# Weights that begin at eleven offsets, and activation blocks 1040 bytes apart

## The chip, the cores and the metric

The kernel runs on one core of one Trainium2 chip. The metric is device time in microseconds of that core, the median of several runs. One execution of the kernel before was profiled, and all rows shown here are from it.

## The reference, cut to what matters

One decoder layer over 256 tokens of width 1024, all in float32. What is computed:

```
h      = rmsnorm(x) ;  q, k, v, u_pool, gate_logits = split(h @ w_in)
attn   = causal attention over q, k (per-head norm, partial rotary), v
pooled = four trailing-mean poolings of u_pool, then a small map
mixed  = sig(g0) * (attn @ w_branch_attn) + sig(g1) * (pooled @ w_branch_pool)
x      = x + mixed @ w_out
up     = causal_depthwise_conv(rmsnorm(x) @ w_up)          # 1024 -> 2 * 2816
out    = x + (silu(up_gate) * up_value) @ w_down           # 2816 -> 1024
```

## The kernel before

Every large product is made of three float32r products: an operand is split into a high part (ScalarE, `high`, L78) and a low part, the difference (VectorE, `low`, L82 or L84), and TensorE adds high·high, high·low and low·high in PSUM (`mm3`, L90 to L92; the same in `down`, L632 to L634, and `project`, L276).

Weights come in chunks of 128 partitions by 2048 numbers (8192 bytes per partition). SyncE loads a chunk into one of four `raw` buffers. `next_high` writes its high part into one of four `whi` buffers and `next_low` the low part into one of four `wlo` buffers, each in two pieces of 1024 columns. The list `order` sets the order of the chunks: q, k, v, p (pooling input), g (gates, 8 chunks), the pool maps, bp and ba (branches), o (output, 4 chunks), then up (22 chunks) mixed with dn (11 chunks).

Activations lie transposed, as 8 blocks (`k`) of 256 tokens: `xhi` and `xlo` for the first half, `hhi` and `hlo` in the same buffers for the feed-forward part. In p, g, o, up and dn a weight tile of 128 by 128 is the stationary operand (an LDWEIGHTS, then the MATMUL), and 256 columns of activations move past it. A chunk of g, o, up or dn is used by 48 such matmuls: g, o and up by 2 feature tiles of 8 blocks and 3 products, dn by 2 rows of blocks, 8 tiles and 3 products. In q, k and v the operands change places: 128 tokens are stationary and 512 weight columns move.

In the built program the buffers follow one another without gaps that matter here: each `whi` and `wlo` buffer begins 64 bytes past a multiple of 128, each tile in it a multiple of 512 bytes later; `xhi`, `xlo` and all other activation operands begin 96 bytes past a multiple of 128, and their blocks are 1024 bytes apart. So before the change every float32r matmul with 256 columns meets one pair of residues modulo 128: 64 for the weights, 96 for the activations.

The program's order on each engine is the order in which the code issues it. After the normalised keys are made, GpSimd does the rotary part of q and k in `norm_evacuate` (L294 to L305), with scratch tiles `ra` and `rb` of two buffers each.

Of the kernel before, what the change touches and what calls it, by code (L numbers as in the profile page):

```python
# [8 lines left out]
F32 = mybir.dt.float32  # L9
F32R = mybir.dt.float32r  # L10
# [4 lines left out]
P = 128  # L15
S = 256
NT = S // P
D = 1024
KD = D // P
H = 8  # L20
# [8 lines left out]
ROPE = 16  # L29
# [3 lines left out]
CH = 2048  # L33
# [17 lines left out]
STAGGER = 1  # L51
AHEAD = 4
FFN_AHEAD = 6
XCUTS = (1, 2, 4, 6, 8)


@with_exitstack
def hybrid_layer_kernel(ctx: ExitStack, tc: tile.TileContext, xq_d, par_d, wkv_d, wpg_d,
# [5 lines left out]
    whi_p = ctx.enter_context(tc.tile_pool(name="whi", bufs=WBUFS))  # L64
    wlo_p = ctx.enter_context(tc.tile_pool(name="wlo", bufs=WBUFS))
    act = ctx.enter_context(tc.tile_pool(name="act", bufs=1))
# [4 lines left out]
    tmp = mixer.enter_context(tc.tile_pool(name="tmp", bufs=2))  # L71
# [5 lines left out]
    def high(hi, src, scale=1.0):  # L77
        nc.scalar.activation(hi, src, AF.Copy, scale=scale)  # L78
# [16 lines left out]
    order = [("q", None)] * 2 + [("k", wkv_d[c]) for c in range(2)]  # L95
# [10 lines left out]
    raws, his, los = {}, {}, {}  # L106
# [14 lines left out]
    def raw(c, sl):  # L121

        return xq[:, 4 * c + sl.start // 512, S:] if order[c][0] == "q" else raws[c][:, sl]
# [10 lines left out]
    def oldest():  # L134

        return next((c for c in range(len(order)) if c not in spent), len(order))

    def next_high():
        if at[0] < len(pieces):
            c, sl, first, _ = pieces[at[0]]  # L140
            if c - oldest() >= WBUFS:
                return
            at[0] += 1
            if first:
                his[c] = whi_p.tile([P, CH], F32R, tag="whi", name=f"hi_{order[c][0]}{c}")
                los[c] = wlo_p.tile([P, CH], F32R, tag="wlo", name=f"lo_{order[c][0]}{c}")
            high(his[c][:, sl], raw(c, sl))

    def next_low(eager=False):
# [9 lines left out]
    def ahead(upto=0):  # L159

        next_high()
        next_low()
        if at[1] - sum(p[0] < used[0] for p in pieces) < upto:
            next_high()
            next_low()
# [14 lines left out]
    gmix = xq_all[:, 0:KD]  # L180
    xq = xq_all[:, KD:].rearrange("p (k c) -> p k c", c=S + AW)
    xT = xq[:, :, 0:S]
    xhi = act.tile([P, KD, S], F32R, tag="xhi", name="xhi")
    xlo = act.tile([P, KD, S], F32R, tag="xlo", name="xlo")
    par = const.tile([P, C_END], F32, name="par")
    scrap = const.tile([P, 1], F32, name="scrap")
    nc.scalar.activation(scrap, ones[:, 0:1], AF.Copy)
# [1 line left out]
    cut = 0  # L189
    for k in XCUTS:  # L190
        end = KD + k * (S + AW)
# [25 lines left out]
    for k in range(KD):  # L217
        if k == 0:
            nc.vector.tensor_scalar(xhi[:, k, :], xT[:, k, :], gmix[:, k:k + 1], None, op0=ALU.mult)
        else:  # L220
            high(xhi[:, k, :], xT[:, k, :], gmix[:, k:k + 1])
        low(xlo[:, k, :], xhi[:, k, :], xT[:, k, :], gmix[:, k:k + 1])
        next_high()
        next_low(eager=True)
# [56 lines left out]
    def norm_evacuate(pt, t, gcol, name):  # L281
        r = rtok1[:, t:t + 1]
        g = par[:, None, gcol:gcol + DH].to_broadcast([P, H, DH])
        p3 = pt.rearrange("p (h d) -> p h d", d=DH)
        qg = tmp.tile([P, 2, 3 * P], F32, tag="big", bufs=4, name=f"qg_{name}{t}")
        qg = qg.rearrange("p a b -> p (a b)")[:, 0:AW].rearrange("p (h d) -> p h d", d=DH)
        q2 = tmp.tile([P, H, DH], F32, tag="q2", bufs=1, name=f"q2_{name}{t}")
        nc.scalar.activation(q2, p3, AF.Square, scale=r)
        nc.vector.scalar_tensor_tensor(qg, p3, r, g, ALU.mult, ALU.mult)
        ss = tmp.tile([P, H], F32, tag="ss", name=f"ss_{name}{t}")  # L290
        nc.vector.tensor_reduce(ss, q2, axis=AX.X, op=ALU.add)
        nc.vector.tensor_scalar(ss, ss, 1.0 / DH, EPS, op0=ALU.mult, op1=ALU.add)
        rh = tmp.tile([P, H], F32, tag="rh", name=f"rh_{name}{t}")
        nc.gpsimd.tensor_tensor(rh, ss, mhalf[:, 0:H], ALU.pow)  # L294
        nc.gpsimd.tensor_tensor(qg, qg, rh[:, :, None].to_broadcast([P, H, DH]), ALU.mult)
        cos = par[:, None, C_COS + t * ROPE:C_COS + (t + 1) * ROPE].to_broadcast([P, H, ROPE])
        sin = par[:, None, C_SIN + t * ROPE:C_SIN + (t + 1) * ROPE]
        ta = tmp.tile([P, H, ROPE], F32, tag="ropea", name=f"ra_{name}{t}")
        tb = tmp.tile([P, H, ROPE], F32, tag="ropeb", name=f"rb_{name}{t}")
        nc.gpsimd.tensor_tensor(ta, qg[:, :, 0:ROPE], cos, ALU.mult)  # L300
        nc.gpsimd.tensor_tensor(tb[:, :, 0:HALF], qg[:, :, HALF:ROPE],
                                sin[:, :, 0:HALF].to_broadcast([P, H, HALF]), ALU.mult)
        nc.gpsimd.tensor_tensor(tb[:, :, HALF:ROPE], qg[:, :, 0:HALF],
                                sin[:, :, HALF:ROPE].to_broadcast([P, H, HALF]), ALU.mult)
        nc.gpsimd.tensor_tensor(qg[:, :, 0:ROPE], ta, tb, ALU.add)  # L305
        return qg
# [18 lines left out]
    def on_k(k):  # L325
        if k % 2 == 1:
            ahead()
        if k == 3:
            stat.append(ps2.tile([P, 2, 512], F32, tag="ps2", name="ps_n1"))
            token_rms(stat[0][:, 0, :], x2, rtok1, "n1")  # L330
            diagonal(rtok1)
            qg.append(norm_evacuate(ptq[0], 0, C_QG, "q"))
        if k == 5:
            qg.append(norm_evacuate(ptq[1], 1, C_QG, "q"))
        if k == 6:
            spread_rms(stat[0][:, 1, 0:S], R1)

    def on_v(k):
        if k % 2 == 1:
            ahead()  # L340
        if k == 1:
            kg.append(norm_evacuate(ptk[0], 0, C_KG, "k"))
        if k == 3:
            kg.append(norm_evacuate(ptk[1], 1, C_KG, "k"))
# [152 lines left out]
    for n in range(2 * KD):  # L497
# [5 lines left out]
        b, c = n // 2, n % 2  # L503
# [30 lines left out]
    tmp = ctx.enter_context(tc.tile_pool(name="ffn", bufs=2))  # L534
# [14 lines left out]
    low(ml[:, KD - 1, :], mh[:, KD - 1, :], gate(KD - 1))  # L549


    hhi = act.tile([P, KD, S], F32R, tag="xhi", name="hhi")
    hlo = act.tile([P, KD, S], F32R, tag="xlo", name="hlo")
    ss2 = tmp.tile([P, S], F32, tag="ss2", bufs=1, name="ss2")

    def tile_part(w, opers, c, ps, ks):
# [56 lines left out]
    def value_done(i, g, uc):  # L613
        taps(uc[0], KF + i, uc[1])
        nc.gpsimd.tensor_tensor(uc[1], g[1], uc[1], ALU.mult)  # L615
        acch[i] = tmp.tile([P, S], F32R, tag="ah", bufs=LAG + 2, name=f"ah{i}")
        accl[i] = tmp.tile([P, S], F32R, tag="al", bufs=LAG + 2, name=f"al{i}")
        high(acch[i], uc[1])
        return uc[1]
# [4 lines left out]
    def down(i, ms):  # L624
        if i % 2 == 0 and i // 2 not in wd:
            wd[i // 2] = chunk("dn")
        hi, lo = wd[i // 2]
        for m in ms:
            sl = slice((i % 2) * D + m * P, (i % 2) * D + (m + 1) * P)
            o = acc[m // 2][:, (m % 2) * S:(m % 2 + 1) * S]  # L630
            first = i == 0 and m % 2 == 0
            nc.tensor.matmul(o, hi[:, sl], acch[i], start=first, stop=False, skip_group_check=True)  # L632
            nc.tensor.matmul(o, hi[:, sl], accl[i], start=False, stop=False, skip_group_check=True)  # L633
            nc.tensor.matmul(o, lo[:, sl], acch[i], start=False, stop=i == KF - 1, skip_group_check=True)  # L634
        if i % 2 == 1 and len(ms) == KD:
            spent.add(next(c for c in his if his[c] is hi))
# [29 lines left out]
    for i in range(1, KF):  # L666
# [11 lines left out]
        if i >= LAG:  # L678
# [4 lines left out]
            down(i - LAG, range(KD))  # L683
            ahead(FFN_AHEAD)
        done = value_done(i, ug, uv)
# [6 lines left out]
    for m in (0, 2, 4, 6, 1, 3, 5, 7):  # L692
        for i in (KF - 2, KF - 1):
            down(i, (m,))
        o = acc[m // 2][:, (m % 2) * S:(m % 2 + 1) * S]
# [75 lines left out]
```

## Time and profile before

| What | us |
|---|---|
| median of 3 runs | 358.66 |
| lowest and highest of them | 357.54, 359.63 |
| the profiled execution's own time | 356.89 |
| its span, first to last instruction | 355.1 |

The span is what the rows below add up to; about 1.8 us of the execution lie around it. "PE" is TensorE's matmuls and "PEld" its weight loads, which overlap them; "DVE" is VectorE, "ACT" ScalarE, "POOL" GpSimd. A matmul's duration in a row is its way through the array, so neighbours overlap; what a matmul costs in a dense stretch is the distance from one start to the next.

### The profile page before, as it was taken

How to read it: one execution, taken by the hardware profiler on the slowest of the kernel's cores; microseconds unless marked ns; L12 is line 12 of the kernel's file. 1: busy time of each engine (PE TensorE's matmuls, PEld its weight loads, DVE VectorE, ACT ScalarE, POOL GpSimd, SP SyncE). 2: the span in 40 equal slices, each digit the busy share in tenths (PEclk: the TensorE clock that was granted, in tenths of full speed). 3: DMA queues.
4: the chain of work that ended last, by engine and by line, in shares of the span. 5: the costliest groups of instructions: out<-in, count | busy, mean ns of one | idle time of the engine just before them, and what ended most of it. 6: DMA issues, size and time to landing. Idle time of an engine off the chain costs nothing.

```text
span 355.1 us, 6775 instructions
## 1 busy us (share of the span) xinstructions
PE 344.3 (97%) x2760; PEld 334.5 (94%) x2760; DVE 255.3 (72%) x401; ACT 195.4 (55%) x311; POOL 101.7 (29%) x127
## 2 busy tenths in 40 slices
PE   8999895999999999999999999999999999999996
PEld 6887794999999999999999999999999999999996
DVE  4879727944677597499789986667777777777743
ACT  5955614636464984566467565555555555556420
POOL 1008999100000006379232222121212121212140
PEclk9999998999999999999999999999999999999999
DMA  7985623244263464075534764646455453642003
GB/s 281 420 341 178 252 90 119 49 173 170 116 236 120 173 258 163 6 293 194 221 117 140 278 236 180 220 145 231 134 222 185 172 228 128 238 132 107 2 0 118
DMA packets 10254, 62.76 MB, mean 177 GB/s; under 512 B 1136, under 2 KB 2288, under 8 KB 3312
## 3 DMA queue, kind: packets, MB, share of 16 engines
q1 hardware_dynamic: 10224, 62.34, 48.3%
q8 instruction: 21, 0.34, 0.4%
q14 instruction: 9, 0.07, 0.1%
HBM read 61.29 MB, written 1.05 MB: 176 GB/s over the span
## 4 chain that ended last, share of the span: by engine, by line
PE 75%; POOL 8%; DVE 8%; DMA 3%; ACT 2%; issue 2%; SPq 1%; POOLq 0%
PE ps_up L91 11%; PE ps_up L90 11%; PE ps_up L92 11%; PE ps_d L633 6%; PE ps_d L632 6%; PE ps_d L634 6%; PE ps_g L90 5%; PE ps_g L91 4%; PE ps_g L92 4%; DMA raw_k<-in_wkv 3%; DVE lo_up L82 2%; DVE hlo L84 2%; POOL rh_k L294 1%; POOL rh_q L294 1%; PE ps_bp L90 1%
## 5 line engine op out<-in xcount | busy, mean ns | idle before, releaser
L91 PE MATMUL ps_up<-hlo,hi_up 128*128 128x256 f32 x352 | 98.5, 280 | 0.2 <-DVE hlo L84 0.2
L90 PE MATMUL ps_up<-hhi,hi_up 128*128 128x256 f32 x352 | 98.7, 280 | 0.0
L92 PE MATMUL ps_up<-hhi,lo_up 128*128 128x256 f32 x352 | 98.4, 280 | 0.0
L91 PEld LDWEIGHTS ps_up<-hlo,hi_up 128*128 128x128 f32 x352 | 66.2, 188 | 0.4 <-DVE hlo L84 0.4
L90 PEld LDWEIGHTS ps_up<-hhi,hi_up 128*128 128x128 f32 x352 | 66.2, 188 | 0.0
L92 PEld LDWEIGHTS ps_up<-hhi,lo_up 128*128 128x128 f32 x352 | 66.2, 188 | 0.0
L82 DVE TENSOR_TENSOR lo_up<-raw_up,hi_up 128x1024 fp32r<-128x1024 f32 x44 | 55.9, 1274 | 6.1 <-ACT hi_up L78 6.1
L615 POOL TENSOR_TENSOR c_v<-c_g,c_v 128x256 f32<-128x256 f32 x22 | 16.3, 740 | 120.7 <-DVE c_v L598 120.7
L633 PE MATMUL ps_d<-al,hi_dn 128*128 128x256 f32 x176 | 49.2, 280 | 0.0
L634 PE MATMUL ps_d<-ah,lo_dn 128*128 128x256 f32 x176 | 49.2, 280 | 0.0
L632 PE MATMUL ps_d<-ah,hi_dn 128*128 128x256 f32 x176 | 49.2, 279 | 0.0
L78 ACT ACTIVATE hi_up<-raw_up 128x1024 fp32r<-128x1024 f32 x44 | 44.9, 1045 | 0.0
L90 PE MATMUL ps_g<-xhi,hi_g 128*128 128x256 f32 x128 | 37.5, 293 | 0.0
L91 PE MATMUL ps_g<-xlo,hi_g 128*128 128x256 f32 x128 | 36.3, 284 | 0.0
L92 PE MATMUL ps_g<-xhi,lo_g 128*128 128x256 f32 x128 | 36.3, 284 | 0.0
L78 ACT ACTIVATE ah<-c_v 128x256 fp32r<-128x256 f32 x22 | 9.2, 418 | 45.9 <-POOL c_v L615 45.9
L634 PEld LDWEIGHTS ps_d<-ah,lo_dn 128*128 128x128 f32 x176 | 33.1, 188 | 0.0
L632 PEld LDWEIGHTS ps_d<-ah,hi_dn 128*128 128x128 f32 x176 | 33.1, 188 | 0.0
L633 PEld LDWEIGHTS ps_d<-al,hi_dn 128*128 128x128 f32 x176 | 33.1, 188 | 0.0
L545 POOL TENSOR_TENSOR xq<-xq 128x256 f32<-128x256 f32 x8 | 7.0, 887 | 74.1 <-issue 70.1
L82 DVE TENSOR_TENSOR lo_dn<-raw_dn,hi_dn 128x1024 fp32r<-128x1024 f32 x22 | 27.8, 1265 | 0.4 <-ACT hi_dn L78 0.4
L603 DVE TENSOR_TENSOR u_v<-ps_up,R 128x256 f32<-128x256 f32 x22 | 9.3, 422 | 26.1 <-PE ps_up L92 26.1
(191 smaller groups left out, 843.7 us busy)
## 6 DMA issues: line engine op xcount, KB each, us to landing
raw_up<-in_wup SPq DMA_DIRECT2D x22, 1024.0 KB, 4.8
raw_dn<-in_wdn SPq DMA_DIRECT2D x11, 1024.0 KB, 4.8
raw_g<-in_wpg SPq DMA_DIRECT2D x8, 1024.0 KB, 4.8
raw_o<-in_wout SPq DMA_DIRECT2D x4, 1024.0 KB, 4.8
xq<-in_xq SPq DMA_DIRECT2D x3, 768.0 KB, 7.3
raw_v<-in_wkv SPq DMA_DIRECT2D x2, 1024.0 KB, 14.0
raw_p<-in_wpg SPq DMA_DIRECT2D x2, 1024.0 KB, 6.3
raw_bp<-in_wbp SPq DMA_DIRECT2D x2, 1024.0 KB, 5.5
```

The costliest lines, as they stand in the source:

```text
L78: nc.scalar.activation(hi, src, AF.Copy, scale=scale)
L82: nc.vector.tensor_tensor(lo, src, hi.bitcast(F32), ALU.subtract)
L84: nc.vector.scalar_tensor_tensor(lo, src, scale, hi.bitcast(F32), ALU.mult, ALU.subtract)
L90: nc.tensor.matmul(out, sh, mh, start=start, stop=False, **kw)
L91: nc.tensor.matmul(out, sh, ml, start=False, stop=False, **kw)
L92: nc.tensor.matmul(out, sl, mh, start=False, stop=stop, **kw)
L294: nc.gpsimd.tensor_tensor(rh, ss, mhalf[:, 0:H], ALU.pow)
L603: nc.vector.tensor_tensor(u, ps[:, 0:S], R2, ALU.mult)
L615: nc.gpsimd.tensor_tensor(uc[1], g[1], uc[1], ALU.mult)
L632: nc.tensor.matmul(o, hi[:, sl], acch[i], start=first, stop=False, skip_group_check=True)
L633: nc.tensor.matmul(o, hi[:, sl], accl[i], start=False, stop=False, skip_group_check=True)
L634: nc.tensor.matmul(o, lo[:, sl], acch[i], start=False, stop=i == KF - 1, skip_group_check=True)
```

## The change

Each `whi` and `wlo` buffer grows by 112 bytes, and the chunk inside begins at one of eleven byte offsets, 0, 64, 4, 32, 8, 96, 16, 48, 80, 112 or 12, by its turn among the chunks of its name. Only chunks of up, dn, g and o are shifted; the high and the low part of a chunk take the same offset. In the built program a buffer takes 8320 bytes, so buffers still begin 64 past a multiple of 128, and the offset adds to that. The activation tiles `xhi`, `xlo`, `hhi` and `hlo` get blocks of 260 numbers, of which 256 are used, so that block `k` begins 16·k bytes later than before modulo 1024. The rotary scratch tiles go from two buffers to one each, which makes room.

```
+SHIFT = (0, 64, 4, 32, 8, 96, 16, 48, 80, 112, 12)
+SPAN = S + 4
...
             if first:
-                his[c] = whi_p.tile([P, CH], F32R, tag="whi", name=f"hi_{order[c][0]}{c}")
-                los[c] = wlo_p.tile([P, CH], F32R, tag="wlo", name=f"lo_{order[c][0]}{c}")
+                name = order[c][0]
+                turn = sum(order[i][0] == name for i in range(c))
+                off = SHIFT[turn % len(SHIFT)] // 4 if name in ("up", "dn", "g", "o") else 0
+                his[c] = whi_p.tile([P, CH + max(SHIFT) // 4], F32R, tag="whi", name=f"hi_{name}{c}")[:, off:off + CH]
+                los[c] = wlo_p.tile([P, CH + max(SHIFT) // 4], F32R, tag="wlo", name=f"lo_{name}{c}")[:, off:off + CH]
...
-    xhi = act.tile([P, KD, S], F32R, tag="xhi", name="xhi")
-    xlo = act.tile([P, KD, S], F32R, tag="xlo", name="xlo")
+    xhi = act.tile([P, KD, SPAN], F32R, tag="xhi", name="xhi")[:, :, 0:S]
+    xlo = act.tile([P, KD, SPAN], F32R, tag="xlo", name="xlo")[:, :, 0:S]
...
-        ta = tmp.tile([P, H, ROPE], F32, tag="ropea", name=f"ra_{name}{t}")
-        tb = tmp.tile([P, H, ROPE], F32, tag="ropeb", name=f"rb_{name}{t}")
+        ta = tmp.tile([P, H, ROPE], F32, tag="ropea", bufs=1, name=f"ra_{name}{t}")
+        tb = tmp.tile([P, H, ROPE], F32, tag="ropeb", bufs=1, name=f"rb_{name}{t}")
...
-    hhi = act.tile([P, KD, S], F32R, tag="xhi", name="hhi")
-    hlo = act.tile([P, KD, S], F32R, tag="xlo", name="hlo")
+    hhi = act.tile([P, KD, SPAN], F32R, tag="xhi", name="hhi")[:, :, 0:S]
+    hlo = act.tile([P, KD, SPAN], F32R, tag="xlo", name="hlo")[:, :, 0:S]
```

The change moves no instruction: on every engine the built program holds the same instructions in the same order with the same semaphore waits, at other addresses. The one place where a wait could have been added is GpSimd's queue, where the rotary part's scratch tiles lose their second buffer. GpSimd's rows there, before (`ra_q` and `rb_q` are the scratch tiles, `qg_q` a half of the queries):

```order
L300 TENSOR_TENSOR ra_q_289<-qg_q_279,par 128x128 [waits DMAHW7_49,Pool_49]
L301 TENSOR_TENSOR rb_q_290<-qg_q_279,par 128x8x8
L303 TENSOR_TENSOR rb_q_290<-qg_q_279,par 128x8x8
L305 TENSOR_TENSOR qg_q_279<-ra_q_289,rb_q_290 128x8x16 [waits Pool_49]
L294 TENSOR_TENSOR rh_q_320<-ss_q_317,mhalf 128x8 [waits DVE_49]
L295 TENSOR_TENSOR qg_q_313<-qg_q_313,rh_q_320 128x512 [waits Pool_49]
L300 TENSOR_TENSOR ra_q_323<-qg_q_313,par 128x128 [waits Pool_49]
```

The same place in the changed program, whose lines stand six further down:

```order
L306 TENSOR_TENSOR ra_q_289<-qg_q_279,par 128x128 [waits DMAHW7_49,Pool_49]
L307 TENSOR_TENSOR rb_q_290<-qg_q_279,par 128x8x8
L309 TENSOR_TENSOR rb_q_290<-qg_q_279,par 128x8x8
L311 TENSOR_TENSOR qg_q_279<-ra_q_289,rb_q_290 128x8x16 [waits Pool_49]
L300 TENSOR_TENSOR rh_q_320<-ss_q_317,mhalf 128x8 [waits DVE_49]
L301 TENSOR_TENSOR qg_q_313<-qg_q_313,rh_q_320 128x512 [waits Pool_49]
L306 TENSOR_TENSOR ra_q_323<-qg_q_313,par 128x128 [waits Pool_49]
```

Only the line numbers differ: the second use of the scratch tiles waits for GpSimd's own earlier work in both.

## Rows read from the trace of the kernel before

**Rows 1.** The page's first part: busy us, share of the span, instructions.

```profile
PE 344.3 (97%) x2760; PEld 334.5 (94%) x2760; DVE 255.3 (72%) x401; ACT 195.4 (55%) x311; POOL 101.7 (29%) x127
```

**Rows 2.** Busy time by stretch: length, engines, TensorE's granted clock, DMA.

```profile
core 0: us, PE busy (x) PEld busy (x) DVE busy (x) ACT busy (x) POOL busy (x), PEclk, DMA share, GB/s
70.00:130.00 60.00, 60.00 (x519) 59.34 (x518) 38.58 (x66) 36.38 (x72) 0.00 (x0) 1.00 0.47 169
130.00:177.00 47.00, 46.41 (x394) 45.95 (x393) 37.39 (x58) 24.62 (x36) 26.35 (x24) 1.00 0.52 189
177.00:345.00 168.00, 168.00 (x1442) 168.00 (x1441) 125.62 (x188) 96.06 (x144) 39.21 (x44) 1.00 0.46 164
```

**Rows 3.** Timeline of TensorE, feed-forward: start, duration, instruction; 1152 starts apart.

```profile
200.46 0.28 PE L90 MATMUL ps_up<-hhi,hi_up 128*128 128x256 f32 x1
...
334.86 0.28 PE L90 MATMUL ps_up<-hhi,hi_up 128*128 128x256 f32 x1
```

**Rows 4.** Timeline of TensorE in the k projection, pairs with 512 columns.

```profile
18.48 0.63 PE L276 MATMUL ps_k<-hi_k,xhi 128*128 128x512 f32 x2
18.95 0.63 PE L276 MATMUL ps_k<-hi_k,xlo 128*128 128x512 f32 x2
...
21.75 0.63 PE L276 MATMUL ps_k<-hi_k,xlo 128*128 128x512 f32 x2
```

**Rows 5.** Timeline of TensorE early in the gates; nine starts apart.

```profile
61.10 0.41 PE L92 MATMUL ps_g<-xhi,lo_g 128*128 128x256 f32 x1
...
63.02 0.42 PE L92 MATMUL ps_g<-xhi,lo_g 128*128 128x256 f32 x1
```

**Rows 6.** Busy time around the gates' first tile, columns as in rows 2.

```profile
54.00:59.00 5.00, 1.27 (x12) 1.03 (x10) 4.43 (x9) 3.33 (x6) 4.77 (x8) 1.00 0.53 184
61.00:63.00 2.00, 2.00 (x11) 2.00 (x11) 1.93 (x4) 0.00 (x0) 1.87 (x5) 0.50 0.00 0
```

**Rows 7.** Timeline of TensorE in the pooling input; 88 starts apart.

```profile
43.04 0.28 PE L91 MATMUL ps_u<-xlo,hi_p 128*128 128x256 f32 x1
...
53.41 0.28 PE L92 MATMUL ps_u<-xhi,lo_p 128*128 128x256 f32 x1
```

**Rows 8.** Weight loads by line and form: busy us, mean ns, idle before.

```profile
L90 PEld LDWEIGHTS ps_up<-hhi,hi_up 128*128 128x128 f32 x352 | 66.2, 188 | 0.0
L276 PEld LDWEIGHTS ps_k<-hi_k,xlo 128*128 128x128 f32 x16 | 3.0, 188 | 0.7
L445 PEld LDWEIGHTS ps_p<-ident,sm 128*128 128x128 f32 x24 | 2.7, 140 | 0.0
```

**Rows 9.** VectorE operations by line and form, columns as in rows 8.

```profile
L598 DVE SCALAR_TENSOR_TENSOR c_v<-u_v,par,c_v 128x254 f32<-128x254 f32 x22 | 10.6, 484 | 0.8
L597 DVE SCALAR_TENSOR_TENSOR c_v<-u_v,par,c_v 128x255 f32<-128x255 f32 x22 | 10.5, 479 | 0.0
L84 DVE SCALAR_TENSOR_TENSOR xlo<-xq,xhi 128x256 fp32r<-128x256 f32 x8 | 3.9, 482 | 1.0 <-ACT xhi L78 0.9
```

**Rows 10.** The chain that ended last, output projection: start, us, what.

```profile
147.91 0.44 DVE xq L564
...
152.43 0.43 issue
152.86 0.84 DVE hlo L84
...
154.48 1.06 ACT hi_o L78
...
157.81 0.33 DVE xq L564
158.15 1.13 DVE lo_up L82
```

## The prediction

> **What bounds the kernel now.** I read the page's busy shares first: TensorE is busy 97% of the span, VectorE 72%, ScalarE 55% [rows 1]. A busy TensorE is not yet a bound, so I read the stretches next. From 70 to 130 us and from 177 to 345 us TensorE has no idle time at all, and from 130 to 177 us it lacks 0.6 us [rows 2]. In 275 of 355 us, then, the time is the number of matmuls times the distance between their starts. Everything else is hidden as long as buffers are filled in time.
>
> So the distance is what to look at. In the feed-forward part two starts that are 1152 matmuls apart (16 rounds of 72: two up tiles of 24 and a down step of 24) lie 134.40 us apart: 116.67 ns each [rows 3]. At the granted full clock, 2.4 GHz, that is 280 cycles for 256 columns, 24 more than one per column. In the k projection with 512 columns, seven pairs take 21.75 − 18.48 = 3.27 us, or 233.6 ns per matmul, 561 cycles, 49 more than one per column [rows 4]. While the clock is granted at half, 1.2 GHz, after TensorE had been busy for 1.27 of 5 us [rows 6], nine starts take 1.92 us: 213.3 ns, which is 256 cycles and none over [rows 5]. The reader is to see three things: there is a loss of 9.4% per column at full clock; it doubles when the columns double, though there is one weight load in either case; at half clock it is gone.
>
> **What the change does, part by part.**
>
> *Instructions and waits.* None is added, removed or reordered on any engine, SyncE's transfers included, and GpSimd's rotary steps wait as before. Losing the second scratch buffer costs 0: both uses stand in one engine's queue, and the second never began before the first had ended.
>
> *Addresses that TensorE reads.* Matmuls with a new address in at least one operand: g 384 and p 96 (re-spaced activations), o 144 (three of four chunks are shifted; mixed activations are not re-spaced), up 1056 (re-spaced), dn 480 (ten of eleven chunks). That is 2160 of 256 columns. The 144 matmuls of q, k and v only get a re-spaced stationary operand; each has a slot of 233 ns for a load that takes 188 ns [rows 4, 8], so I cost them at 0.
>
> What a new residue does to the distance between starts no row shows: in this trace every operand begins at a multiple of 32 bytes. I bound it. From below: the loss goes away, and the distance becomes half of the half-clock distance, 213.3 / 2 = 106.7 ns [rows 5]. That is −10.0 ns × 2160 = −21.6 us. From above: an access that does not begin on a 16-byte multiple runs at half rate, as the half-clock rows do, 213.3 ns. Offsets 4, 8 and 12 are such; they fall on 2 chunks of g, 1 of o, 6 of up and 3 of dn, 12 chunks with 48 matmuls each: 576 × 96.7 ns = +55.7 us. A price between comes from the one stretch at full clock that departs from 116.67: in the pooling input 88 starts take 10.37 us, 117.8 ns each [rows 7]. Its 1.1 ns on all 2160 matmuls would be +2.5 us.
>
> I take 0, for two reasons. First, the loss follows the moving columns and not the loads: a collision of weight reads with activation reads that costs a fixed amount per load would be the same 10 ns at 512 columns, and it is 20 [rows 3, 4]. The moving operand is read straight through 1024 or 2048 bytes, so it passes all residues wherever it begins; a new start can alter the edges, not the middle. Second, in k the residues are exchanged (weights move, activations stand), and the loss per column is the same within the rounding of the rows.
>
> The Trainium skill ("TensorE: Matmul & The Clock Gate", section Back-to-back issue gap) gives a distance of columns / 2.4 plus 2.5 ns for a warm stream, 109.2 ns at 256 columns; the trace disagrees, with 116.67 ns [rows 3]. By that page 7.5 ns per matmul are to be had, and if residues were what withholds them, the sum would be an estimated −16 us. The same skill ("SBUF — State Buffer", section Who interferes with whom) says that TensorE reads its moving operand and its weights through two ports that are independent, which speaks against such a gain; the 512-column rows agree with that, as the loss is not one per load.
>
> *Addresses that VectorE and ScalarE use.* They write the shifted chunks and re-spaced blocks. VectorE's taps already read and write 4 bytes (L597) and 8 bytes (L598) off: 479 and 484 ns, against 482 ns for the low part of a block that begins on a 32-byte multiple [rows 9]. So VectorE: 0. ScalarE has no odd start in the trace. Its cover is wide in the feed-forward part, where it is busy 96 of 168 us and VectorE 126 [rows 2]. Without cover it would count only in the output projection, where a chain of ScalarE and VectorE runs beside TensorE from 147.9 to 174 us [rows 10]; there one chunk of o and one of up have offset 4, four ScalarE passes of 1.06 us, so even 20% more is 0.8 us. I take 0, with 0 to +0.8 as bounds; a gain is excluded, since these passes have no loss that alignment explains.
>
> The sum: 356.9 us for the profiled execution (355.1 of span and 1.8 around it) plus 0. That execution was 1.8 us below the median of the three runs, so as a median I say 358.6 us.
>
> **The rivals.**
>
> *Slower: odd starts stretch the weight loads.* A load takes 188 ns and must begin every 116.67 ns [rows 3, 8], so loads already overlap, and how much of the slot one occupies is not shown. If it is nearly all, an extra access at each odd start pushes the slot. For it: 188 ns is more than the 140 ns of the transposes' loads [rows 8], so loads of this kind are not at their fastest, and 117.8 ns in the pooling input shows that the slot can be pushed. Against it: the load is 188 ns in k too, where the slot is twice as long, so nothing squeezes it now. It decides from 1.8 us, which is 0.83 ns on all 2160 matmuls or 3.1 ns on the 576 with odd starts. Small form, the 1.1 ns above: 358.6 + 2.5 = 361. Large form, half rate on odd starts: 358.6 + 55.7 = 414.
>
> The Trainium skill ("Advanced Engine Details and Errata", section SBUF Cachelines) speaks for this rival: memory lines have 16 bytes, and at least two hits on a line are needed to hide its latency, so a start 4 or 12 bytes off leaves a line with a single hit at one end. No row here shows it.
>
> *Faster: the residues did collide.* All 256-column matmuls meet the pair 64 and 96, and the loss is there in all of them. If it belongs to that pair, most of the new pairs escape it. All of it gives 358.6 − 21.6 = 337; half of the pairs gives 348. For it: a steady 9.4% with no other cause named in the trace. Against it: the two reasons above.
>
> *The change does nothing to what TensorE fetches.* That is my forecast.
>
> **How the numbers follow.** About 0.5%, 1.8 us, is what a measurement of this kernel can tell from no change; its three runs span 2.1 us. My forecast, no change: 0.62, at 358.6, between 357 and 360.4. Slower: 0.24, of which 0.12 the small form up to 368, and 0.12 beyond it. Faster: 0.14, of which 0.06 down to 352 and 0.08 beyond. The range of 352 to 368 holds 0.62 + 0.12 + 0.06 = 0.80. The one likeliest case would have 357 to 360.4 alone.
>
> **What would show it.** In the profile after: the distance between matmul starts in up and dn, chunk by chunk. If I am right, all eleven offsets show 116.67 ns, the loads 188 ns, and the high and low passes their old durations. If odd starts cost, the up chunks of turn 2, 4, 10, 13, 15 and 21 show a longer distance than their neighbours, and nothing else does. If the residues collided, the distances fall, and differ between offsets or between blocks of one tile. The forecast is wrong if the mean distance in the feed-forward part moves by more than 0.8 ns; and if the distance holds but the time moves, the output projection's chain is where to look.

## The result, and the profile after

The changed kernel took 361.06 us (median of 5 runs, 359.84 to 361.24) against 358.48 us (357.54 to 359.63) for the kernel before: a ratio of 1.0066, 95% interval 1.0038 to 1.0094. It is slower by 0.66%, where no change was forecast. The profiled execution took 359.84 us with a span of 358.1 us, 3.0 us more than before.

The page's first part of the changed kernel answers to [rows 1]; the three stretches after it (columns as in [rows 2], their limits moved with the work) answer to [rows 2].

```profile
PE 347.5 (97%) x2760; PEld 338.3 (94%) x2760; DVE 255.1 (71%) x401; ACT 195.5 (55%) x311; POOL 102.5 (29%) x127
```

```profile
70.00:130.00 60.00, 60.00 (x513) 59.34 (x512) 37.83 (x65) 35.90 (x72) 0.00 (x0) 1.00 0.45 165
130.00:178.00 48.00, 47.60 (x402) 47.34 (x401) 38.18 (x60) 25.15 (x37) 26.34 (x24) 1.00 0.53 189
178.00:348.00 170.00, 170.00 (x1441) 170.00 (x1441) 125.21 (x187) 96.09 (x144) 39.81 (x44) 1.00 0.46 162
```

The counts of instructions are the same, and TensorE is the only engine that works clearly longer, by 3.2 us. It is still never idle in the long stretches: in the first it gets through 513 matmuls instead of 519, and in the last the same work takes 2 us more. So the distance from start to start has grown. TensorE's timeline shows it at the same two matmuls as [rows 3], 1152 starts apart:

```profile
201.40 0.28 PE L93 MATMUL ps_up<-hhi,hi_up 128*128 128x256 f32 x1
...
337.57 0.28 PE L93 MATMUL ps_up<-hhi,hi_up 128*128 128x256 f32 x1
```

136.17 us for 1152, or 118.20 ns each, where it was 116.67. On the 1584 matmuls of up and dn these 1.53 ns are 2.4 us of the 3.0. The new distance from start to start is not one number. The last two chunks of dn, in the same timeline, first of offset 112, then of offset 12 (only the first of each three matmuls is shown; 24 starts lie between the first two rows, 27 between the others):

```profile
345.70 0.28 PE L638 MATMUL ps_d<-ah,hi_dn 128*128 128x256 f32 x1
...
348.50 0.28 PE L638 MATMUL ps_d<-ah,hi_dn 128*128 128x256 f32 x1
...
351.01 0.28 PE L638 MATMUL ps_d<-ah,hi_dn 128*128 128x256 f32 x1
...
354.25 0.28 PE L638 MATMUL ps_d<-ah,hi_dn 128*128 128x256 f32 x1
```

That is 116.7 ns in one chunk and 120.0 ns in the next. Chunk means, taken from the starts in the same trace: offsets 4 (o, 119.9 ns) and 16 (dn, 119.8 ns) are as slow as 12, and 8 (dn, 117.7 ns) is faster than 16, so multiples of 16 are not spared. Every other group is as before; the groups by line and form, which answer to [rows 8, 9]:

```profile
L93 PEld LDWEIGHTS ps_up<-hhi,hi_up 128*128 128x128 f32 x352 | 66.2, 188 | 0.0
L604 DVE SCALAR_TENSOR_TENSOR c_v<-u_v,par,c_v 128x254 f32<-128x254 f32 x22 | 10.6, 483 | 0.8
L85 DVE TENSOR_TENSOR lo_up<-raw_up,hi_up 128x1024 fp32r<-128x1024 f32 x44 | 55.8, 1273 | 6.1 <-ACT hi_up L81 6.1
L81 ACT ACTIVATE hi_up<-raw_up 128x1024 fp32r<-128x1024 f32 x44 | 44.9, 1045 | 0.0
```

The weight loads still take 188 ns, and VectorE and ScalarE write the shifted chunks in 1273 and 1045 ns (1274 and 1045 before).

### The profile page after: what moved, and what is told of

Read it like the earlier page. It is cut to its first block, busy times and chain, and to the rows that moved or that the text cites. A ratio compares the mean times of both kernels' runs of the same rounds, so it can differ in the third digit from the quotient of the medians.

```text
span 358.1 us, 6775 instructions
## 1 busy us (share of the span) xinstructions
PE 347.5 (97%) x2760; PEld 338.3 (94%) x2760; DVE 255.1 (71%) x401; ACT 195.5 (55%) x311; POOL 102.5 (29%) x127
## 4 chain that ended last, share of the span: by engine, by line
PE 75%; POOL 8%; DVE 8%; DMA 3%; ACT 2%; issue 2%; SPq 1%; POOLq 0%
PE ps_up L94 11%; PE ps_up L95 11%; PE ps_up L93 11%; PE ps_d L639 6%; PE ps_d L640 6%; PE ps_d L638 6%; PE ps_g L93 5%; PE ps_g L95 4%; PE ps_g L94 4%; DMA raw_k<-in_wkv 3%; DVE lo_up L85 2%; DVE hlo L87 2%; POOL rh_k L300 1%; POOL rh_q L300 1%; PE ps_bp L93 1%
## 5 line engine op out<-in xcount | busy, mean ns | idle before, releaser
L85 DVE TENSOR_TENSOR lo_up<-raw_up,hi_up 128x1024 fp32r<-128x1024 f32 x44 | 55.8, 1273 | 6.1 <-ACT hi_up L81 6.1
L81 ACT ACTIVATE hi_up<-raw_up 128x1024 fp32r<-128x1024 f32 x44 | 44.9, 1045 | 0.0
```

The costliest lines, as they stand in the source:

```text
L85: nc.vector.tensor_tensor(lo, src, hi.bitcast(F32), ALU.subtract)
```

## The experiments

The theory after this: a matmul's moving stream and the next weight load meet in the memory, and the *distance* of their addresses (weight minus moving address, modulo 256) sets how often. The rival: only starts off a multiple of 16 bytes cost. From here on a distance in bytes, or a bare number such as 224, is the one between addresses; in ns it is the one from start to start.

**The change in parts.** Three kernels: the first two are edits of the changed kernel and keep its single scratch buffers, the last takes the activation spacing alone into the kernel before.

```
# e_pad: the larger weight buffers alone
-SPAN = S + 4
+SPAN = S
-off = SHIFT[turn % len(SHIFT)] // 4 if name in ("up", "dn", "g", "o") else 0
+off = 0 if name in ("up", "dn", "g", "o") else 0

# e_shift: larger buffers and offsets
-SPAN = S + 4
+SPAN = S

# e_space, from the kernel before
+SPAN = S + 4
-xhi = act.tile([P, KD, S], F32R, tag="xhi", name="xhi")
+xhi = act.tile([P, KD, SPAN], F32R, tag="xhi", name="xhi")[:, :, 0:S]
...
```

> The larger weight buffers alone: no chunk is shifted inside, activations 1024 bytes apart, so buffers begin 8320 bytes apart and high and low parts no longer have one residue modulo 1024. Theory: part of the loss comes back, +0.5 to +1.5 us against before, with distances of 117 to 118.8 ns in some chunks. Rival (odd starts): 0, all distances 116.67 ns.

Ratio 1.0020 (1.0003 to 1.0037), median 358.43 us. With every start as aligned as before, some dn chunks went to 118.0 ns and some up chunks to 118.7, while others stayed at 116.7. A buffer of 8320 bytes is an odd multiple of 128, so every second buffer puts its chunk 128 bytes off modulo 256: where TensorE never waits, the chunks at distance 224 are those that stayed, the ones at 96 those that slowed. The rival said 0 there.

> The weights' half of the change alone: larger buffers and the eleven offsets, activations 1024 bytes apart. Theory: +1.5 to +3 us against before, spread over offsets that are multiples of 16 as well. Rival: the whole +2.4 us, and only in the twelve chunks at offsets 4, 8 and 12.

Ratio 1.0094 (1.0072 to 1.0117), median 361.24 us, 3.2 us above the kernel before, where 1.5 to 3 were expected. The weights' half alone costs about as much as the whole change (the two intervals overlap). The mean time from start to start per chunk lies between 115.6 ns (dn, offset 96) and 123.2 ns (up, offset 8). The slow chunks are not the odd ones alone: g at offset 16 takes 120.0 ns, up at 32 takes 119.7 and 119.9.

> The activations' half alone: blocks 1040 bytes apart, weight buffers as before. Theory: +0.5 to +1.5 us, in g, p and up only, as distances that change from block to block in one tile; dn and o stay at 116.67 ns. Rival: 0 everywhere, since all starts stay multiples of 16.

Ratio 1.0047 (1.0025 to 1.0068), median 359.33 us. TensorE's timeline at the two matmuls of [rows 3]:

```profile
201.25 0.28 PE L91 MATMUL ps_up<-hhi,hi_up 128*128 128x256 f32 x1
...
337.14 0.28 PE L91 MATMUL ps_up<-hhi,hi_up 128*128 128x256 f32 x1
```

That is 117.96 ns over up and dn together; on average 118.5 in up and 116.8 in dn, whose operands did not move. The theory named these places. The parts do not add up (0.47% and 0.94% against 0.66% together), which fits the theory: both halves change one quantity, the distance.

**Maps of the distance.** Kernels that leave the layer out: one weight block, one activation block, and groups of 30 matmuls of 256 columns (16 of 512), each group with another weight address.

```
def group(name, n, count, a, w):
    ps = mm.tile([P, 512], F32, tag="mm", name=f"ps_{name}")
    for i in range(count):
        nc.tensor.matmul(ps[:, 0:n], wgt[:, w:w + P], mov[:, a:a + n], start=i == 0, stop=i == count - 1)
...
for d in range(0, 1024, 16):
    group(f"n{d}", 256, GROUP, 0, d // 4)
...
```

> Matmuls alone: 30 in a row of 256 columns with one moving address and one weight address, for 64 weight addresses 16 bytes apart and 12 at other multiples of 4, then 16 in a row of 512 columns for 16 addresses 32 bytes apart. The layer itself is left out. Theory (the two streams that TensorE reads meet in the memory, and how often depends on the distance of their addresses): the distance between starts differs between multiples of 16, repeats with some period, and some groups lie below 116.67 ns, the best near 109. Rival (only starts off a 16-byte multiple cost): all 64 multiples of 16 show 116.67 ns and only the 12 others show more, 119 to 120. With 512 columns, theory: some groups below 233.3 ns; rival: all at 233.3.

> Matmuls alone again, the layer left out: 256 columns at all 64 distances of weight address minus moving address from 0 to 252 bytes in steps of 4, then 7 of these with both addresses 100 bytes later, then 512 columns at all 64. Theory (the distance alone counts, modulo 256): the multiples of 16 repeat the first map (0: 120.0, 64: 113.3, 112: 120.3, 224: 116.7 ns), the 7 shifted ones equal their unshifted ones within 0.3 ns, and the mean over all 64 is about 118, above 116.67. Rival (the absolute start counts): the 7 shifted ones differ.

The distance between starts, from the records of the first map (256 columns, mean without a group's first eight):

```
weight minus moving address, bytes   ns from start to start
  0  256  512  768                   120.0  120.0  120.0  120.0
 64  320  576  832                   113.3  113.3  113.3  113.3
112  368  624  880                   120.3  120.3  120.3  120.2
192  448  704  960                   117.8  117.8  117.8  117.8
224  480  736  992                   116.7  116.7  116.7  116.7
```

Within this map the values repeat every 256 bytes, multiples of 16 differ by up to 7 ns, and no other engine was at work. That refutes the rival's flat line. The best is 113.3, not the 109 that the theory allowed for. Distance 224 is that of the kernel before, and shows its 116.67 ns. With 512 columns the groups range from 226.6 ns (distance 0) to 234.3 (distance 96), and distance 32, that of q, k and v, shows 233.6 as in [rows 4]. The maps also account for the changed kernel. By the addresses in the built program its eleven dn chunks stand at the distances 96, 32, 100, 128, 232, 192, 112, 16, 176, 208 and 236, and the means of the first ten lie within 0.6 ns of one of the two maps: 119.5 ns at 100, 117.7 at 232 and 116.7 at 208, for instance, where the second map has 120.0, 117.8 and 116.7.

In the second map two statements of the theory failed. The multiples of 16 did not all repeat: 128, 144 and 240 show 118.7, 120.0 and 120.1 ns, where the first map has 120.0, 118.1 and 117.1. And with both addresses 100 bytes later, seven distances show 119.9 to 123.3 ns, where six of them unshifted show 113.3 to 120.1 and the seventh, 24, 122.0. So the distance alone is not the whole of it. The shift makes the moving operand begin 4 bytes past a multiple of 16, which may be the reason, but only this one shift was tried, and the groups ahead differed too. In the change no moving operand begins so.

**The kernel before with one other distance.** Nothing but unused bytes ahead of the activation buffers:

```
+GAP = 40     # 160 bytes; 56 for gap224
+gap = ctx.enter_context(tc.tile_pool(name="gap", bufs=1))
 act = ctx.enter_context(tc.tile_pool(name="act", bufs=1))
+gap.tile([P, GAP], F32, name="gap")
```

> The same with 224 unused bytes: weight minus activation address becomes 0 modulo 256 for 256 columns. Theory: 120.0 ns from start to start, +3.33 x 2460 = +8.2 us, ratio 1.023. Rival: 0.

Ratio 1.0172 (1.0144 to 1.0200), median 364.20 us. Timeline of TensorE, the two matmuls of [rows 3]:

```profile
203.08 0.28 PE L93 MATMUL ps_up<-hhi,hi_up 128*128 128x256 f32 x1
...
341.32 0.28 PE L93 MATMUL ps_up<-hhi,hi_up 128*128 128x256 f32 x1
```

138.24 us for 1152 starts, 120.0 ns each, as the map has it for distance 0. No operand starts less aligned than before. The whole is 6.2 us slower and not 8.2, in part because the forecast left out q, k and v: their 512-column matmuls came to distance 0 too and got faster, 226.7 ns each in k where [rows 4] has 233.6, about 1 us on the 144.

> The kernel before with 160 unused bytes ahead of the activation buffers and nothing else: weight minus activation address becomes 64 modulo 256 in all 2460 matmuls of 256 columns, and 192 in the 144 of 512. Theory: 113.33 ns from start to start where it was 116.67, so -3.33 x 2460 = -8.2 us, and 229.3 for 233.4 ns, -0.6 us: about 349.5 us, ratio 0.976; less where another engine becomes the bound. Rival (residues cost only where starts are odd or blocks are re-spaced): 0.

Here the theory was incomplete. Of seven executions three took 350.9 to 351.3 us and four 357.9 to 359.0. The ratio of 0.9804 (0.9758 to 0.9849) is of the three; the median of all seven, 357.85 us, is no gain over the 357.95 of the kernel before. The profile is of one of the four. Its timeline, once in the output projection (nine starts apart), once at the two matmuls of [rows 3]:

```profile
142.75 0.28 PE L93 MATMUL ps_out<-mh,hi_o 128*128 128x256 f32 x1
...
143.77 0.28 PE L93 MATMUL ps_out<-mh,hi_o 128*128 128x256 f32 x1
```

```profile
200.48 0.28 PE L93 MATMUL ps_up<-hhi,hi_up 128*128 128x256 f32 x1
...
336.16 0.28 PE L93 MATMUL ps_up<-hhi,hi_up 128*128 128x256 f32 x1
```

1.02 us for nine is 113.3 ns, as forecast, but the feed-forward part runs at 117.8 ns with the same distance, and at a granted clock of 1.00 as before. There are two patterns for one distance. Whether the way in decides is the question of a third map, with 60 matmuls a group:

```
for d in path:      # each of 0, 52, 64, 88, 224 entered from each of the others
    group(f"{word[d]}_after_{prev}", 256, LONG, 0, d // 4)
    prev = word[d]
...
```

> Matmuls alone, the layer left out: the distances 0, 52, 64, 88 and 224, 60 matmuls of 256 columns in a row, each distance entered from each of the other four and from seven matmuls of 512 columns; then the sixteen multiples of 16 in order. Theory (a distance allows a few locked patterns, and the way in chooses one): 64 shows 113.33 ns from some and 117.77 from others, 224 shows 116.67 and 117.77, 0 only 120.0. Rival (one pattern for each distance, and the second pattern in the layer comes of the other engines' accesses): every distance shows one value whatever came before.

Timeline of TensorE: start, duration, group, and the count of matmuls; a group ends where the next row starts.

```profile
24.47 7.01 PE L80 MATMUL ps_fiftytwo_after_zero<-mov,wgt 128*128 128x256 f32 x60
31.32 7.36 PE L80 MATMUL ps_zero_after_fiftytwo<-mov,wgt 128*128 128x256 f32 x60
38.52 7.23 PE L80 MATMUL ps_sixtyfour_after_zero<-mov,wgt 128*128 128x256 f32 x60
45.59 7.36 PE L80 MATMUL ps_zero_after_sixtyfour<-mov,wgt 128*128 128x256 f32 x60
52.78 7.17 PE L80 MATMUL s_eightyeight_after_zero<-mov,wgt 128*128 128x256 f32 x60
59.78 7.36 PE L80 MATMUL s_zero_after_eightyeight<-mov,wgt 128*128 128x256 f32 x60
...
80.83 6.96 PE L80 MATMUL sixtyfour_after_fiftytwo<-mov,wgt 128*128 128x256 f32 x60
87.63 6.96 PE L80 MATMUL fiftytwo_after_sixtyfour<-mov,wgt 128*128 128x256 f32 x60
94.43 6.96 PE L80 MATMUL ghtyeight_after_fiftytwo<-mov,wgt 128*128 128x256 f32 x60
101.23 6.97 PE L80 MATMUL ftytwo_after_eightyeight<-mov,wgt 128*128 128x256 f32 x60
...
173.84 7.37 PE L80 MATMUL ps_fiftytwo_after_wide<-mov,wgt 128*128 128x256 f32 x60
181.05 1.77 PE L80 MATMUL ps_wide<-mov,wgt 128*128 128x512 f32 x7
```

Distance 64 takes 7.07 us after distance 0 (117.8 ns) and 6.80 after 52 (113.3). Distance 88 takes 7.00 us (116.7) or 6.80. Distance 52 takes 6.85 and 6.80, but after the 512-column group, in the last row, its 60 starts are 120.0 ns apart. Distance 0 takes 7.20 us, 120.0 ns, in all six cases. Distance 224 showed no second value, though the theory had forecast one. So three of the five have more than one pattern with no other engine at work; the rival, one value each, is refuted. That the way in chooses is likely and not proved, since each way was run once; in the first map the four passes through the same sequence gave the same values within 0.1 ns. The sixteen multiples of 16 in order close the run, from the first to the last of them:

```profile
206.78 7.36 PE L80 MATMUL ps_step_a<-mov,wgt 128*128 128x256 f32 x60
...
312.98 7.36 PE L80 MATMUL ps_step_p<-mov,wgt 128*128 128x256 f32 x60
```

Fifteen groups, 900 matmuls, take 106.20 us: 118.0 ns on average. That is what spreading over many places buys. The first map has the same order with 30 matmuls a group, and 96, 128 and 240 differ all the same: 118.6, 120.0 and 117.1 ns there, 117.3, 118.7 and 120.0 here. So the distance of the group ahead does not decide alone.

**Versions that beat both kernels.** They were built before the map of ways in. One offset for all chunks but q, k and v:

```
+OFF = 84 // 4      # 120 // 4 in off88
+ROOM = 64
+off = 0 if order[c][0] in ("q", "k", "v") else OFF
-his[c] = whi_p.tile([P, CH], F32R, tag="whi", name=f"hi_{order[c][0]}{c}")
+his[c] = whi_p.tile([P, CH + ROOM], F32R, tag="whi", name=f"hi_{order[c][0]}{c}")[:, off:off + CH]
...           # the same for los[c]
```

> The same with an offset of 84 bytes, a distance of 52 modulo 256, which settled in 113.33 ns after six matmuls in the second map and at once in the first. Theory: -8.2 us in every execution. Rival with two patterns: executions near 350 and near 358. Odd-start rival: slower than before.

Four of six executions took 350.6 to 351.5 us, two 356.6 and 356.7; median 351.15; the ratio of the four is 0.9784 (0.9751 to 0.9818). The mean of all six is 352.8 us against 358.6 for the eleven executions of the kernel before on the same chip, 1.6% less. Timeline, the two matmuls of [rows 3]:

```profile
198.74 0.28 PE L92 MATMUL ps_up<-hhi,hi_up 128*128 128x256 f32 x1
...
329.30 0.28 PE L92 MATMUL ps_up<-hhi,hi_up 128*128 128x256 f32 x1
```

130.56 us for 1152, 113.33 ns each, with each of these weight tiles beginning 4 bytes past a multiple of 16. For weight operands the odd-start rival is refuted outright: this is the fastest kernel of the study.

> One offset of 120 bytes for every chunk but q, k and v, in weight buffers with 256 bytes of room, activations as before: weight minus activation address is 88 modulo 256 in all 2460 matmuls of 256 columns. Theory (the distance fixes the pattern that the two streams settle in, and in the map 88 settled in 113.33 ns within four matmuls): -3.3 x 2460 = -8.2 us in every execution, ratio 0.977. Rival (every distance has a slow pattern too, as 64 has 117.77 ns): executions differ, some near 350, some near 358. Odd-start rival: slower than before, since all weights start 8 bytes off a multiple of 16.

Four of six took 351.5 to 352.9 us, two 356.5 and 357.4; median 352.51; the ratio, without the 357.4, is 0.9850 (0.9799 to 0.9902). The profiled one runs the output projection at 116.7 ns and nearly all of up and dn at 113.3. "In every execution" was wrong for both offsets: four of six executions of each came near the forecast. The slower ones were not profiled; that a slower pattern held parts of them is inferred from gap160.

## Why the prediction was wrong

- *What bounds the kernel.* Right: the time still is the number of matmuls times the distance of their starts.
- *No instruction, no wait, no cost on VectorE and ScalarE.* Right, by the unchanged counts and durations above, and the weight loads stayed at 188 ns.
- *"What a new residue does to the distance … I take 0".* This is the step that failed. Its first reason was that the loss follows the moving columns, not the loads, so that a new start could alter only the edges. The maps show that the whole stream changes pace with the distance of the two addresses, with 512 columns as with 256: by 1.53 ns on average in the feed-forward part of the changed kernel, where the prediction had named 0.8 as the sign of being wrong, and from 113.3 to 120.3 ns between the distances of the first map. Nor is the doubling a law: at distance 0 the loss above one column per cycle is 13.3 ns with 256 columns (120.0) and 13.3 ns with 512 (226.6). The 10 and 20 ns that the prediction compared belong to two different distances, 224 and 32. The second reason was that k, with exchanged residues, has the same loss. Its distance of 32 happens to show 233.6 ns; the maps have 226.6 at others, 0 among them. Two agreeing points were taken for a law.
- *The count of addresses.* The residues were taken modulo 128, and by that the larger buffers moved nothing. Modulo 256 they move every second chunk, also in bp and ba, which the 2160 leave out; e_pad shows what this alone costs, 0.2%.
- *The size.* The 2160 matmuls times 1.1 ns that priced the small slower case, +2.5 us, come close to the measured +2.6, but by luck: its mechanism, odd starts, is refuted by gap224 and off52. The 117.8 ns in the pooling input [rows 7], from which the price came, was 1.1 ns above the same kernel's other stretches at the same distance of 224; that it is a second pattern of that distance fits map3, where three other distances have one, but no map reproduced it.
- *The faster rival* named the right quantity, the pair of residues, and both reasons against it fell. It erred on where the kernel stood. The pair of residues before, at 116.67 ns, is better than the 118.0 of the sixteen multiples of 16, so spreading over many pairs loses. What gains is one good pair.
- *The Trainium skill's two independent ports* ("SBUF — State Buffer", section Who interferes with whom), cited for a gain being unlikely: in effect the runs disagree, as the first map goes from 113.3 to 120.3 ns by the address of the weights alone. The Trainium skill's formula behind the 109.2 ns for 256 columns ("TensorE: Matmul & The Clock Gate", section Back-to-back issue gap) is given there for an isolated matmul and not for a stream of weight loads and matmuls, so it was no measure of what this kernel could gain. No group of the maps reached it.

Open: what in the memory makes 256 bytes the period; why a distance has the values it has (236 took 120.0 ns in the last dn chunk of the changed kernel and 117.8 in the second map; in e_shift 232 took 123.2 in up, where the second map has 117.8); and what decides the way in from execution to execution in gap160, off52 and off88. That the weight load is the colliding partner is inferred: moving the weights' address alone changes the distance between starts, and nothing else read it.

## What to carry to other kernels

When float32r matmuls with a weight load each start evenly but wider apart than one column per cycle, look at the distance of the weight and activation addresses. A map with 30 to 60 matmuls at each distance tells the price; enter each distance from several others, since one way in can miss a second pattern. A few unused bytes ahead of one buffer then set the distance for the whole kernel, as in gap160 and gap224. Choose one good distance and keep it, by making all strides multiples of the period, here 256 bytes; spreading operands over many offsets buys the average, here 118.0 ns. A steady loss in all the stretches of one kernel says nothing of its cause while all of them share one address relation.

## What the runs showed that was not expected

One address relation can run at several speeds. Distance 64 showed 113.3 or 117.8 ns and held the first through 60 matmuls of the third map, the second through the whole feed-forward part of gap160; that this is why executions of one program fell near 351 or near 358 us is inferred, as one slow execution of gap160 was profiled and no fast one. Distance 96 showed 117.3, 118.0 and 118.7 ns in different chunks of e_pad alone. The transition takes a few matmuls: in the first map the group at distance 64 had its 113 ns by the third, in the third map distance 52 after distance 0 by the eleventh.
